# Two mixers with dense steps moved ahead of four products, and the first split block of a feed-forward half in another PSUM bank

## The chip, the cores and the metric

One core of one Trainium2 chip runs the whole program in one launch. The metric is the device time in microseconds, the median of the runs of a kernel. Engines are named as in the profile: PE (TensorE's matmuls), PEld (its weight loads), DVE (VectorE), ACT (ScalarE), POOL (GpSimd), SP (SyncE, which here only issues loads).

## The reference, cut to what matters

Two layers on 256 positions of width 1024, in float32. Each layer is a gated feed-forward half, a token mixer, and a second gated feed-forward half, each after a root-mean-square norm that the conditioning vector scales and shifts.

```python
for l in range(DEPTH):
    h = adaln_pre(x, norm_g[l, 0], shift, scale)
    x = x + 0.5 * gate * swiglu(h, ffn1_w13[l], ffn1_w2[l])
    h = adaln_pre(x, norm_g[l, 1], shift, scale)
    p = dict(zip(names, jnp.split(h @ w_in[l] + b_in[l], splits, axis=-1)))
    y = concat(rms_norm(nsa_mixer(...)), rms_norm(short_conv_mixer(...)), gated_deltanet(...), mlstm_mixer(...))
    x = x + gate * (y @ w_out[l])
    h = adaln_pre(x, norm_g[l, 2], shift, scale)
    x = x + 0.5 * gate * swiglu(h, ffn2_w13[l], ffn2_w2[l])
```

The feed-forward width is 2816, 22 blocks of 128. The mixer has four head groups: sparse attention, a short convolution, a gated delta rule (which needs the inverse of a triangular matrix), and an mLSTM.

## The kernel before, in words

**Feed-forward halves** (class `Half`). Features lie on the partitions and the 256 positions on the free axis. Each block f has three weight tiles of 128x1024: two for the up products (parts 0 and 1) and one for the down product (part 2). A weight tile w is split into a rounded high part `w_..h` (ACT, `high`) and a rest `w_..l` (DVE or POOL, `low`), and a product is three matmuls (`mm3`): high by high, high by low, low by high. The first three blocks of a half (`PRE`) are made unsplit, before the norm's root is known, in the six banks `e0` to `e5`; the root comes through the products `ms` (sum of squares) and `rs` (the roots spread over the partitions), and DVE multiplies it in afterwards (`rooted`: `sl<-e,rsS`). Block 3 (`self.pre`) is the first split block, `ab3`; it is the first pass of the loop in `run`. Each pass there loads and splits the weights of block f+2, runs the 48 matmuls of `ab{f}`, gates it (`gated`: ACT's SiLU `sl<-ab`, then DVE's product `sl<-sl,ab`, then the split into `g`), and adds earlier blocks into the four output banks `y0` to `y3` (`down`: 24 matmuls of a block, six in each bank, in the order y0, y1, y2, y3). The first pass adds block 0. The seam from one half or mixer to the next comes four times: into the first half (`first=True`), and into three others, where `first` is false.

**PSUM banks.** There are eight, in three groups: `c` and `y` with three each, `ab` with two. A tile takes a bank of its group that is free, and its first writer waits until the last readers of the bank's former tile are done. At the three later seams `e0`, `e1`, `e2` are in `c`, `e3` and `e4` in `ab`, `e5`, `ms` and `rs` in `y`. The outputs `y0`, `y1`, `y2` are in `y`, and `y3` is in `ab`.

**What sets the order.** Through the mixers and the seams each engine is held to the order in which the code is written (`InOrder.switch(True)`). The loop in `run` is outside of that: there the framework that builds the program lays the instructions itself, by its own estimate of durations and with the written order as the priority, and each engine then runs its list in that order.

**The mixer** (`mixer`). Its small products depend on chains of small DVE and ACT operations. Between them the code puts pieces of dense work: `step(name, n)` issues the next n products of the input projection (`dq`, `dk`, `c` and so on) or of the output projection (`W3`), 128x128 by 128x256 in float32. The profile counts each such product as two matmul rows. `placed_on_all(name)` reads a finished bank out; for `W3.0` to `W3.3` (four steps each) that is two DVE operations on `xT`. The places that the change touches are lines 1417 (`p_bc`), 1562 (`kq(3)`, `kq(2)`, `scored(0, 0)`), 1654 (`decay_d(0)`), 2043 (`step("W3", 3)`), 2070 (`turned_y(1)`) and 803 (the bank of `ab{f}`). All instructions pass through one recording helper, so every row has line 198.

Of the kernel before, what the change touches and what calls it, by code (L numbers as in the profile page):

```python
# [181 lines left out]
def trunk(ctx: ExitStack, tc: tile.TileContext, a: dict, out: bass.AP, dbg=None):  # L182
# [34 lines left out]
    def mm(o, lhsT, rhs, start=True, stop=True):  # L217
        return pe.matmul(o, lhsT, rhs, start=start, stop=stop, skip_group_check=True)
# [3 lines left out]
    def P(name, tag):  # L222
        return pp.tile([128, 512], F32, tag=tag, bufs=PBUFS[tag], name=name)

    def TT(name, tag, dtype=F32):
        return wk.tile([128, 512], dtype, tag=tag, bufs=BUFS[tag], name=name)
# [67 lines left out]
    def C(n):  # L294
        o, s = CO[n]
        return cst[:, o:o + s]
# [82 lines left out]
    def ada_step(n=1, after=None, q=pool, each=False, tag="ty"):  # L379
        for _ in range(n):  # L380
            ada_load(q, tag)
            ada_use(after, each)
# [182 lines left out]
    def grown(p, l, s, d):  # L565
        c = d % 2
        dve.scalar_tensor_tensor(xT[:, d], p[:, c * T:c * T + T], modG[:, l, s, d:d + 1], xT[:, d],
                                 op0=ALU.mult, op1=ALU.add)
# [27 lines left out]
    class Half:  # L596
# [200 lines left out]
        def run(self, n_ada, first=False):  # L797
            FT = ("c", "ab", "c", "c") if first else ("c", "c", "ab", "c")
            done = 0
            for f in range(self.pre, NF):  # L800
                self.unit(f + AHEAD, range(2))
                self.unit(f + AHEAD, range(2, 3), pool)
                p = P(f"ab{f}", FT[f % 4])
                for half in range(2):
                    for k in range(KD):
                        self.up(f, p, half, k, start=(k == 0))
                g = self.gated(f, p)
                i, m = f - self.pre - 1, NF - 5 - self.pre
                ada_step(n_ada * (i + 1) // m - n_ada * i // m if 0 <= i < m else 0, g, sync if first else pool)
                if first and f in LATE:  # L810
                    LATE[f](g)
                if f == self.pre:
                    self.y = [P(f"y{i}", "y" if i < 3 else "ab") for i in range(4)]
                while done < max(f - 1 - (f == self.pre), 0) and done < NF - TAIL:
                    for d in range(8):
                        self.down(done, d)
                    done += 1
            while done < NF - TAIL:
                for d in range(8):
                    self.down(done, d)  # L820
                done += 1
# [3 lines left out]
    def mixer(l, a1, a2):  # L825
# [40 lines left out]
        def hf(t, u):  # L866
            return t[:, u * T:u * T + T]

        def v2(t):
            return t.rearrange("p (j t) -> p j t", j=2)  # L870
# [4 lines left out]
        def hr(u):  # L875
            return slice(64 * u, 64 * u + 64)
# [27 lines left out]
        def placed_on(n, u, o):  # L904
            nonlocal tok, kr, qr, DQ, DK, og, zb, zS, cs, bs
            m = n + str(u)
            if n == "k":
                kr = TT("kr", "tp") if u == 0 else kr
                biased(hf(kr, u), o, ("ksw", "kvc")[u])
            elif n == "aq":  # L910
                qr = TT("qr", "tp") if u == 0 else qr
                biased(hf(qr, u), o, m)
            elif n == "dq":
                DQ = TT("DQ", "tp") if u == 0 else DQ
                biased(hf(DQ, u), o, m)
            elif n == "dk":
                DK = TT("DK", "tp") if u == 0 else DK
                dve.tensor_scalar(hf(DK, u), o, bcol(m), 0.125, op0=ALU.add, op1=ALU.mult)
            elif n == "o":
                og = TT("og", "tp") if u == 0 else og  # L920
                tanh_half(hf(og, u), o, m)
            elif n == "z":
                zb, zS = (TT("zb", "td"), TT("zS", "tp")) if u == 0 else (zb, zS)
                biased(hf(zb, u), o, m)
                tanh_half(hf(zS, u), o, m)
            elif n == "c":
                cs = TT("cs", "tp") if u == 0 else cs
                biased(hf(cs, u), o, m)
            elif n == "x":
                dve.scalar_tensor_tensor(upad[:, u, 2:], o, bcol(m), hf(cs, u), op0=ALU.add, op1=ALU.mult)  # L930
            elif n == "b":
                bs = TT("bs", "tp") if u == 0 else bs
                biased(hf(bs, u), o, m)
# [54 lines left out]
        def step(name, n=1):  # L988
            if name not in going:
                going[name] = dense(name)  # L990
            for _ in range(n):
                next(going[name], None)
# [11 lines left out]
        def placed_on_all(n):  # L1004
            p = held["banks"].pop(n)
            if n[0] == "W":
                i = int(n[-1])
                grown(p, l, 1, 2 * i)
                grown(p, l, 1, 2 * i + 1)
            elif n == "h":  # L1010
                held["hidS"] = wk.tile([128, 512], F32, tag="hid", bufs=1, name="hidS")
                act.copy(held["hidS"], p)
            else:
                for u in range(2):
                    placed_on(n, u, hf(p, u))
# [30 lines left out]
        def taps(n, u):  # L1046
            j = 2 * "kqv".index(n) + u
            gp, o = held["gp" + n], hf(cvs[n], u)
            w = PA(l, "gconv")[:, 4 * j:4 * j + 4]
            dve.tensor_scalar(o, gp[:, u, 0:T], w[:, 0:1], None, op0=ALU.mult)  # L1050
            for i in range(1, 4):
                dve.scalar_tensor_tensor(o, gp[:, u, i:i + T], w[:, i:i + 1], o, op0=ALU.mult, op1=ALU.add)
# [10 lines left out]
        def kq(h):  # L1063
            r = hr(h % 2)
            p = held["kq", h] = P(f"kq{h}", "c")
            mm(p, KQ[r, h // 2, 0, 0:128], KQ[r, h // 2, :, :])
# [12 lines left out]
        def kr_scaled(u):  # L1079
            for q in range(2):  # L1080
                h = 2 * q + u
                dve.scalar_tensor_tensor(AP1[:, h], held["kr", u][:, q], Dk[:, 1, h:h + 1],
                                         seg1[:, h, None, :].to_broadcast([128, 2, 128]), op0=ALU.mult, op1=ALU.mult)
# [110 lines left out]
        def scored(b, t):  # L1194
            K, n = KB[:, b], 128 * (t + 1)
            for u in range(2):
                held["s", b, t, u] = P(f"s{b}{t}{u}", "y")[:, :2 * n].rearrange("p (q s) -> p q s", q=2)
            for q in range(2):
                for u in range(2):
                    mm(held["s", b, t, u][:, q], qT[hr(u), q, t * 128:t * 128 + 128], K[hr(u), :n])  # L1200
# [213 lines left out]
        placed_on_all("k")  # L1414
        act.copy(glh, gl)

        p_bc = P("bc", "y")
        mm(p_bc[:, 0:8], C("ut"), lf.rearrange("p t h -> p (t h)"), stop=False)
        mm(p_bc[:, 4:8], ones, lf[:, 0], start=False)
        step("dq0")  # L1420
        step("dq1", 4)
        step("dq1")
        taps("k", 1)
        step("dq1")
# [136 lines left out]
        for b in range(2):  # L1561
            act.copy(KB[hr(1 - b), b], KB[hr(b), b])
        kr_scaled(0)
        kq(3)
        kq(2)
        scored(0, 0)
        step("c1", 2)
        taps("v", 1)
        kr_scaled(1)
        placed_on_all("b")  # L1570
# [69 lines left out]
        def decay_d(q):  # L1640
            p = P(f"mw{q}", "y")
            for u in range(2):
                h = 2 * q + u
                for i in range(2):
                    mm(p[:, u * T:u * T + T], identR[:4, h:h + 1].to_broadcast([4, 128]), nMs[i], start=(u == 0 and i == 0), stop=False)
            mm(v2(p)[:, :, 0:128], identR, negR[:, None, :].to_broadcast([128, 2, 128]), start=False)
            held["mw", q] = p

        def decayed(q):
            for u in range(2):  # L1650
                h = 2 * q + u
                act.activation(W0[:, h], held["mw", q][:, u * T:u * T + T], AF.Exp, bias=aa[:, 0, h:h + 1])

        decay_d(0)
        inv_r(1)
        turned(0, 1, 1)
        step("dk0")
        inv_u(0)
        inv_n(1)
        step("dk0")  # L1660
# [379 lines left out]
        for t in range(2):  # L2040
            act.activation(F(f"tmpn{t}", "ta"), acc[:, t * T:t * T + T], AF.Square, accum_out=ss[:, t:t + 1])
        step("W3")
        step("W3", 3)
        p_u2 = P("u2", "c")
        for h in range(4):
            mm(p_u2[:, 64 * h:64 * h + 64], Tt[1][:, h * 128:h * 128 + 128], vp[:, 1, h])
# [8 lines left out]
        def turned_y(t):  # L2055
            p = held["yAT", t] = P(f"yAT{t}", "y")
            for u in range(2):
                tr(p[:, u * 128:u * 128 + 128], acc[:, t * T + u * 128:t * T + u * 128 + 128], ident)
# [7 lines left out]
        for h in range(4):  # L2066
            mm(oC[:, 64 * h:64 * h + 64], AP0[h // 2][:, h % 2, 1, 0:128], U[:, 0, h])
            mm(oC[:, T + 64 * h:T + 64 * h + 64], AP0[h // 2][:, h % 2, 1, 128:], U[:, 0, h], stop=False)
            mm(oC[:, T + 64 * h:T + 64 * h + 64], AP1[:, h, 1, :], U[:, 1, h], start=False)
        turned_y(1)  # L2070
        placed_on_all("W3.1")
        step("W3", 4)
        sqo = TT("sqo", "tc")
        act.activation(sqo, oC, AF.Square)
        xo = SM([128, 2, 4], "xo", "smc")
# [4 lines left out]
        dve.tensor_tensor(v8(no), v8(oC), ro[:, :, :, None].to_broadcast([128, 2, 4, 64]), op=ALU.mult)  # L2080
        placed(1)
        dump("yA", yA)
        step("W3", 4)
        turned_y(0)
        p_oc = turn_back(no, "oCt", "c")
        placed(0)
# [116 lines left out]
```

## Time and profile before

| | |
|---|---|
| median of 3 runs | 1202.23 us |
| the runs | 1198.28, 1202.23, 1204.82 us |
| the profiled execution's own time | 1201.21 us |
| its span | 1199.4 us |
| mean granted TensorE clock | 0.997 |
| PE busy | 1169.1 us (97% of the span) |
| DVE, ACT, POOL busy | 68%, 39%, 23% |

The span runs from the first instruction to the last; the 1.8 us around it are part of the time. PE is busy in nearly all of the span, so the table is read by what PE waits for. A time in the trace is microseconds from the span's start. In a row of the timeline the first two numbers are start and duration, and what stands in brackets is the idle time of that engine just before and what ended it. The mixers lie at about 222 to 418 us and 804 to 1001 us, the three later seams at 418 to 446, 612 to 639 and 1001 to 1029 us.

### The profile page before, as it was taken

The page shows a single profiled execution, that of the slowest core. Times are in us where ns is not written, and L with a number is a line of the kernel's source. Part 1 is how long each engine was busy: PE and PEld are TensorE (multiplying, and loading weights), DVE is VectorE, ACT ScalarE, POOL GpSimd, SP SyncE. Part 2 cuts the span into 40 slices and gives each one's busy share as a digit, 9 for nine tenths or more (in the row PEclk, how much of TensorE's full clock was granted, in tenths as well). Part 3 has the DMA queues.
Part 4 walks back from the last instruction along what each step waited for, and adds up shares of the span by engine and source line. Part 5 has one row for each costly group of instructions (what it writes and reads, how often), then busy time and mean ns, then how long its engine had stood idle before and what let it go on. Part 6 is the DMA issues. An engine that isn't in the chain of part 4 may idle for free.

```text
span 1199.4 us, 21138 instructions
## 1 busy us (share of the span) xinstructions
PE 1169.1 (97%) x8374; PEld 1081.3 (90%) x8374; DVE 815.9 (68%) x1543; ACT 472.7 (39%) x829; POOL 276.9 (23%) x233
## 2 busy tenths in 40 slices
PE   4899999999999999999999999999999999999998
PEld 4799999977779889999999999998866998999998
DVE  6678976358877568888647777734796774765653
ACT  4444454222322354444445444432122334544441
POOL 0023323102100133343321334230201002332321
PEclk9999999999999999999999999999999999999999
DMA  9899985566564338988646787655656532666551
GB/s 327 315 318 329 365 306 190 178 223 195 195 244 140 121 123 288 311 313 291 224 173 229 248 280 265 211 212 176 211 176 248 173 123 71 224 236 228 179 192 50
DMA packets 75444, 266.96 MB, mean 223 GB/s; under 512 B 8559, under 2 KB 9839, under 8 KB 75201
## 3 DMA queue, kind: packets, MB, share of 16 engines
q1 hardware_dynamic: 66096, 232.52, 56.0%
q0 software_dynamic: 8960, 32.88, 8.4%
q8 instruction: 66, 1.08, 0.3%
q14 instruction: 34, 0.28, 0.1%
q10 hardware_dynamic: 288, 0.19, 0.1%
HBM read 264.50 MB, written 2.24 MB: 222 GB/s over the span
## 4 chain that ended last, share of the span: by engine, by line
PE 87%; DVE 7%; DMA 3%; ACT 1%; issue 1%; SPq 0%; DVEq 0%; ACTq 0%
PE ab L198 34%; PE y L198 20%; PE e L198 8%; PE po L198 2%; PE p_td L198 2%; PE pw L198 2%; DVE aw L198 2%; PE hid L198 1%; PE p_o L198 1%; PE p_dk L198 1%; DMA we<-in_ffn_dram 1%; PE p_z L198 1%; PE p_aq L198 1%; DMA aw<-in_adaw_dram 1%; PE p_x L198 1%; PE pv L198 1%
## 5 line engine op out<-in xcount | busy, mean ns | idle before, releaser
L198 DVE SCALAR_TENSOR_TENSOR aw<-aw,cond 128x1024 f32<-128x1024 f32 x144 | 252.0, 1750 | 8.8 <-DMA aw<-in_adaw_dram 8.7
L198 POOL TENSOR_TENSOR w_2l<-w,w_2h 128x1024 fp32r<-128x1024 f32 x71 | 175.0, 2464 | 355.6 <-ACT w_2h L198 349.1
L198 PE MATMUL y<-g,w_2h 128*128 128x256 f32 x1408 | 256.5, 283 | 0.0
L198 PEld LDWEIGHTS y<-g,w_2h 128*128 128x128 f32 x1408 | 218.9, 191 | 0.9 <-issue 0.9
L198 PE MATMUL y<-g,w_2l 128*128 128x256 f32 x704 | 199.2, 283 | 0.0
L198 PE MATMUL ab<-hH,w_0h 128*128 128x256 f32 x600 | 168.8, 281 | 1.3 <-DVE sl L198 1.3
L198 PE MATMUL ab<-hH,w_0l 128*128 128x256 f32 x600 | 168.7, 281 | 0.1
L198 PE MATMUL ab<-hH,w_1l 128*128 128x256 f32 x600 | 168.5, 281 | 0.0
L198 PE MATMUL ab<-hH,w_1h 128*128 128x256 f32 x600 | 168.0, 280 | 0.0
L198 PE MATMUL ab<-hL,w_0h 128*128 128x256 f32 x600 | 167.0, 278 | 0.0
L198 PE MATMUL ab<-hL,w_1h 128*128 128x256 f32 x600 | 166.8, 278 | 0.0
L198 PEld LDWEIGHTS y<-g,w_2l 128*128 128x128 f32 x704 | 134.9, 192 | 0.1
L198 DVE TENSOR_TENSOR w_1l<-w,w_1h 128x1024 fp32r<-128x1024 f32 x75 | 98.5, 1313 | 53.2 <-ACT w_1h L198 52.4
L198 ACT CAST w_2h<-w 128x1024 fp32r<-128x1024 f32 x88 | 91.7, 1047 | 109.1 <-PE ab L198 103.8
L198 ACT CAST w_1h<-w 128x1024 fp32r<-128x1024 f32 x75 | 79.0, 1053 | 119.0 <-PE ab L198 96.5
L198 PEld LDWEIGHTS ab<-hH,w_0h 128*128 128x128 f32 x600 | 113.1, 188 | 2.1 <-issue 2.1
L198 PEld LDWEIGHTS ab<-hL,w_0h 128*128 128x128 f32 x600 | 113.1, 188 | 0.0
L198 PEld LDWEIGHTS ab<-hH,w_0l 128*128 128x128 f32 x600 | 112.6, 188 | 0.3 <-DVE w_0l L198 0.3
L198 PEld LDWEIGHTS ab<-hH,w_1h 128*128 128x128 f32 x600 | 112.8, 188 | 0.0
L198 PEld LDWEIGHTS ab<-hL,w_1h 128*128 128x128 f32 x600 | 112.8, 188 | 0.0
L198 PEld LDWEIGHTS ab<-hH,w_1l 128*128 128x128 f32 x600 | 112.6, 188 | 0.0
L198 DVE TENSOR_TENSOR sl<-sl,ab 128x256 f32<-128x256 f32 x75 | 31.5, 420 | 107.6 <-ACT sl L198 107.6
(444 smaller groups left out, 1887.6 us busy)
## 6 DMA issues: line engine op xcount, KB each, us to landing
w<-in_ffn_dram SPq DMA_DIRECT2D x238, 512.0 KB, 4.4
aw<-in_adaw_dram SPq DMA_DIRECT2D x88, 512.0 KB, 5.0
aw<-in_adaw_dram POOLq DMA_DIRECT2D x56, 512.0 KB, 5.0
we<-in_ffn_dram SPq DMA_DIRECT2D x18, 512.0 KB, 4.4
wh<-in_cw_dram SPq DMA_DIRECT2D x16, 512.0 KB, 3.6
wwo<-in_wout_dram SPq DMA_DIRECT2D x16, 512.0 KB, 3.6
we<-in_ffn_dram SPq DMA_DIRECT2D x16, 256.0 KB, 7.0
wtd<-in_wtd_dram SPq DMA_DIRECT2D x8, 412.0 KB, 5.0
```

Source lines behind the costliest of these rows:

```text
L198: r = f(*args, **kw)
```

## The change

In the first pass of `run`, in the three halves with `first` false, `ab3` takes a bank of the group `y` in place of one of `c`. In both mixers: one step of `dq0` and one of `dq1` go ahead of the products `bc`; the products `s` of `scored(0, 0)` and two steps of `c1` go ahead of `kq(3)` and `kq(2)`; one step of `dk0` goes ahead of `decay_d(0)`; one step of `W3` goes from ahead of the product `u2` to the group ahead of `turned_y(0)` and the product `oCt`, and four steps of `W3` are written ahead of the read-out of `W3.1` rather than behind it. The number of steps stays the same.

```diff
@@ class Half, run
-                p = P(f"ab{f}", FT[f % 4])
+                p = P(f"ab{f}", "y" if f == self.pre and not first else FT[f % 4])
@@ mixer
+        step("dq0")
+        step("dq1")
         p_bc = P("bc", "y")
         mm(p_bc[:, 0:8], C("ut"), lf.rearrange("p t h -> p (t h)"), stop=False)
         mm(p_bc[:, 4:8], ones, lf[:, 0], start=False)
-        step("dq0")
-        step("dq1", 4)
+        step("dq1", 3)
         step("dq1")
@@
         kr_scaled(0)
+        scored(0, 0)
+        step("c1", 2)
         kq(3)
         kq(2)
-        scored(0, 0)
-        step("c1", 2)
         taps("v", 1)
@@
+        step("dk0")
         decay_d(0)
         inv_r(1)
         turned(0, 1, 1)
-        step("dk0")
         inv_u(0)
@@
         step("W3")
-        step("W3", 3)
+        step("W3", 2)
         p_u2 = P("u2", "c")
@@
         turned_y(1)
+        step("W3", 4)
         placed_on_all("W3.1")
-        step("W3", 4)
         sqo = TT("sqo", "tc")
@@
         placed(1)
-        step("W3", 4)
+        step("W3", 5)
         turned_y(0)
         p_oc = turn_back(no, "oCt", "c")
```

## Rows read from the trace of the kernel before

**Rows 1.** The page: span, and busy time of the engines.
```profile
span 1199.4 us, 21138 instructions
PE 1169.1 (97%) x8374; PEld 1081.3 (90%) x8374; DVE 815.9 (68%) x1543; ACT 472.7 (39%) x829; POOL 276.9 (23%) x233
```

**Rows 2.** The waits of PE: waiter, releaser, us in total, times, longest.
```profile
PE kq L198 <- DVE AP L198: 1.3, 2, 0.7
PE ab L198 <- DVE sl L198: 1.3, 2, 0.7
PE oCt L198 <- DVE no L198: 1.1, 2, 0.5
PE bc L198 <- DVE lf L198: 0.8, 2, 0.5
PE mw L198 <- DVE nMl L198: 0.8, 2, 0.4
```

**Rows 3.** Timeline of PE at the seam after the first mixer.
```profile
440.66 0.35 PE L198 MATMUL ab<-hH,w_0h 128*128 128x256 f32 x1 [0.66 <-DVE sl L198]
...
446.35 0.40 PE L198 MATMUL y<-g,w_2h 128*128 128x256 f32 x2
```

**Rows 4.** Timeline of DVE behind that seam.
```profile
449.69 3.82 DVE L198 TENSOR_TENSOR w_2l<-w,w_2h 128x1024 fp32r<-128x1024 f32 x2 [0.67 <-ACT w_2h L198]
453.43 0.41 DVE L198 TENSOR_TENSOR sl<-sl,ab 128x256 f32<-128x256 f32 x1
453.76 1.22 DVE L198 TENSOR_TENSOR w_2l<-w,w_2h 128x1024 fp32r<-128x1024 f32 x1
```

**Rows 5.** The tile sl from 440 to 456 us: duration ns min/median/max.
```profile
L198 DVE SCALAR_TENSOR_TENSOR sl<-sl,sh x3: 470/470/2325, 441.6 to 444.0; 128x256 f32<-128x256 f32 x3
```

**Rows 6.** Timeline of DVE behind the other two seams: the product that ends ab3.
```profile
642.07 0.41 DVE L198 TENSOR_TENSOR sl<-sl,ab 128x256 f32<-128x256 f32 x1
...
1035.88 0.41 DVE L198 TENSOR_TENSOR sl<-sl,ab 128x256 f32<-128x256 f32 x1
```

**Rows 7.** The chain that ended last: start us, us, what.
```profile
642.11 5.66 PE ab L198 x48
...
1028.96 2.87 PE y L198 x24
1031.84 5.66 PE ab L198 x48
```

**Rows 8.** Timeline of PE in the first half's start.
```profile
41.42 5.84 PE L198 MATMUL e<-hF,we 128*128 128x256 f32 x18 [4.31 <-ACT hF L198]
```

**Rows 9.** Busy time by stretch: PE, PEld, DVE, ACT, POOL, granted clock, DMA share, GB/s.
```profile
41.40:47.00 5.60, 5.58 (x18) 4.63 (x19) 5.11 (x11) 2.57 (x7) 0.00 (x0) 0.70 0.90 302
```

**Rows 10.** Timeline of DVE and PE around the products bc, first mixer.
```profile
271.66 0.16 DVE L198 TENSOR_SCALAR lf<-sp 128x8 f32<-128x8 f32 x1
...
271.88 0.39 PE L198 MATMUL bc<-lf,cst 128*128 128x8 f32 x2 [0.51 <-DVE lf L198]
```

**Rows 11.** Timeline of PE and DVE around the products kq, first mixer.
```profile
288.66 1.13 PE L198 MATMUL kq<-KQ 64*128 64x512 f32 x4
...
297.34 0.69 PE L198 MATMUL kq<-KQ 64*128 64x512 f32 x1 [0.67 <-DVE AP L198]
...
308.42 0.88 DVE L198 SCALAR_TENSOR_TENSOR E<-s,ra_y,BT 128x256 f32<-128x256 f32 x2 [0.64 <-PE s L198]
```

**Rows 12.** Timeline of PE at decay_d(0), first mixer.
```profile
320.58 0.38 PE L198 MATMUL mw<-nMh,cstR 4*128 4x256 f32 x1
```

**Rows 13.** Timeline of DVE and PE around the product oCt, first mixer.
```profile
397.69 0.87 DVE L198 SCALAR_TENSOR_TENSOR xT<-pw,modG,xT 128x256 f32<-128x256 f32 x2
...
399.46 3.62 PE L198 MATMUL pw<-yD,wwo 128*128 128x256 f32 x16
...
400.07 0.69 DVE L198 TENSOR_REDUCE xo<-sqo 128x8 f32<-128x512 f32 x1 [1.50 <-ACT sqo L198]
...
403.83 0.66 PE L198 MATMUL oCt<-cst,no 128*128 128x128 f32 x4 [0.53 <-DVE no L198]
```

## The prediction

> **What bounds the kernel now.** I read the page first: PE is busy in 1169.1 of 1199.4 us [rows 1], so nearly all of the time is PE's own work, and a change that only reorders work can win no more than PE waits. The second view is the list of PE's waits [rows 2]. Five of them are on DVE inside the stretches that the change touches: kq 1.3, ab 1.3, oCt 1.1, bc 0.8 and mw 0.8 us, each over two places. Together that is 5.3 us, and it is the most that the change can win: 0.44% of the time. What can be told from no change here is about 0.5%, 6.0 us of the median of 1202.23. The third view is the timeline at each place, to see what is late next.
>
> The sum is made against the profiled execution, 1201.2 us (span 1199.4 and 1.8 around it). It lies 1.0 below the median of the three runs, well inside their scatter.
>
> **The bank of ab3: what it removes.** At the seams after the two mixers the first matmul of ab3 waits 0.66 us for DVE to read e0, whose bank it takes [rows 2, 3]. In the group y the banks of ms and rs have long been read, so the wait goes: 1.3 us together. At the seam between the layers there is no such wait, and nothing to win.
>
> **The bank of ab3: what it adds.** The group y has three banks, and y0, y1 and y2 are to take all three in the same pass. One of them now belongs to ab3 until DVE's product `sl<-sl,ab` has read it. So the third output bank, y2 (matmuls 13 to 18 of block 0's 24), has a new wait: on the gating of ab3. Before the change nothing waited for that product.
>
> How late is it? At the first seam y0 starts at 446.35 [rows 3] and would start 0.66 earlier. A down matmul takes 2.87 us / 24 = 0.12 [rows 7]. y0 and y1 are done 1.4 us after the start, at 447.1. The product on ab3 runs at 453.43 for 0.41 us [rows 4] and ends at 453.84; with the 0.14 us between DVE's end and PE's start y2 can begin at 453.98. Nothing in that product's delay depends on PE: it stands on DVE behind a pair of w_2l splits of 3.82 us [rows 4], and before them a gate of 2.33 us [rows 5].
>
> What does PE do meanwhile? PE runs its list in order, and here the list is the scheduler's, not the written one: on DVE `sl<-sl,ab` runs ahead of the third w_2l [rows 4], which is written before the loop. So I expect y3, whose bank is in another group, and matmuls of ab4 ahead of y2, as many as the scheduler thinks fit before the product ends. If it plans with durations of operations that run alone, it is too early by what the shared work costs on the chip: the gate takes 2.33 in place of 0.47 [rows 5], 1.86 too much, and the pair 3.82 in place of 2 x 1.22 [rows 4], 1.4 too much. It would then plan the product's end for about 453.84 - 3.3 = 450.5, and PE would stand from 450.5 on the clock of before (449.9 on its own, being 0.66 ahead) until 453.98. Against before that is a loss of 453.98 - 450.5 = 3.5 us, the 0.66 already used up.
>
> The bounds: if all 48 matmuls of ab4 (5.66 us [rows 7]) go ahead of y2, the wait is hidden and 0.66 is won; if y2 keeps its place behind y1, PE stands from 447.1 on, or 447.8 on the clock of before, and loses 6.2. I take 3.5, since the planned place rests on rows of the same stretch. At the second mixer's seam the product starts at 1035.88 and the down matmuls at 1028.96 [rows 6, 7], the same distance within 0.2 us: 3.4. Between the layers the product ends at 642.48 and ab4 starts at 642.11 [rows 6, 7], with no such contention: 0.2. Sum 7.1 us (bounds -1.3 and +13). Nothing absorbs it: behind the seam PE runs without waits to the half's end, so a late PE stays late.
>
> **The clock.** In the first half PE waited 4.3 us, up to 41.42 [rows 8], and in the 5.6 us after it the granted clock was 0.70 in the mean [rows 9]: between full (2.4 GHz) and half (1.2 GHz) that is 3.4 us at half, 1.7 us of work lost. The two new waits would be about 4.1 us each, just below that. Ends 0 and 3.4; I take one loss in the two, 1.7, because the nearest row is a little longer than they are.
>
> The Trainium skill, TensorE: Matmul & The Clock Gate, Part 1, goes further: half rate is the array's default, and an idle stretch brings it back. The trace agrees after the wait of rows 8. By that rule both waits would pay, 3.4 in place of 1.7.
>
> **bc.** PE waits 0.51 us for lf in the first mixer [rows 10], 0.3 in the second by the total [rows 2]. Two steps now go ahead; eight cost 3.62 [rows 13], so two take 0.9 and cover the wait: 0.8 won. dq1 was next in any case and its weights are there. DVE reads bc only after other work, so nothing becomes late.
>
> **kq.** kq(2) waits 0.67 for its bank, which DVE still reads [rows 11]; with s and two steps of c1 ahead (over 1.3 us) that wait is covered. kq(3) and kq(2) also come next to each other, as the pair kq(1), kq(0) does, whose four rows take 1.13 us together [rows 11], against 0.69 for a single row: so PE may gain up to 1.3 there. But it runs into the next wait: mw waits 0.4 for nMl already [rows 2], an operation that stands on DVE behind one long run of work. PE can gain past that point only what DVE gains, and DVE's one idle spot between is the 0.64 us in which it waits for s of scored(0, 1) [rows 11]. So 0.6 for each mixer, 1.2 together; bounds 0 and 2.6.
>
> **dk0.** The products mw of decay_d(0) start with no wait marked [rows 12]; the wait mw of rows 2 is at another place, so a step ahead of them covers nothing. 0. If the cover were missing behind it, inv_u(0) would wait at most the one step, 0.45: bounds -0.9 and 0.
>
> **oCt.** One step (0.45) goes from ahead of u2 to ahead of oCt, which waits 0.53 for no [rows 13]. That alone would win 0.4. But u2 and all behind it come 0.45 earlier with only seven steps done, so the eighth, the last that W3.1 needs, now falls behind turned_y(1): it runs in the first 0.45 us of the row of sixteen, 399.01 to 399.46 (that row starts 0.45 earlier than 399.46). On DVE the read-out of W3.1 is still ahead of the reduction xo, so it moves from 397.69, where it filled idle time, to about 399.6, and takes 0.87 [rows 13]. The reduction starts at about 400.45 in place of 400.07, and the chain of small operations to no, and oCt, follow 0.4 later. PE has the same number of steps ahead of oCt and gets there at the same time. The wait grows from 0.53 to 0.9: 0.4 lost in each mixer, 0.8 together; bounds 0.8 lost and 0.9 won.
>
> **Sum.** 1201.2 + 7.1 (banks) + 1.7 (clock) - 0.8 (bc) - 1.2 (kq) + 0 (dk0) + 0.8 (oCt) = 1208.8 us. Without loss of clock 1207.1, with both 1210.5.
>
> **Rivals.** *ab4 hides the wait* (chance 0.16), the one on the other side: not slower. Its place is the list of PE behind y1. y2's first matmul would come at or after 453.9 if nearly the whole of ab4 goes ahead; the deciding point is how late the scheduler believes the product on ab3 to be, and it is from about 45 of the 48 matmuls on that the loss is under 0.4 us. For it: the product's true end, 453.84, is 6.1 us behind PE's arrival at y2, and a scheduler that knew it would fill all of that. Against: the excess of rows 4 and 5 comes from work on other engines at the same time. Time: 1201.2 - 1.3 - 0.8 - 1.2 + 0.8 = 1198.7, and 1196 if oCt also wins what its step covers and the mw wait goes.
>
> *y2 keeps its written place* (chance 0.08): the matmuls of y3 and ab4 stay behind it, and each of the two waits costs 6.2, the third about 2; both clocks fall. 1201.2 + 14.4 + 3.4 - 1.2 = 1218. Against it is the order on DVE in rows 4.
>
> *Both clocks fall* (chance 0.15): the forecast with 1210.5; for it the one row of its length [rows 8, 9].
>
> *The change does not do what it says* (chance 0.06): ab3 gets the bank of e5, which DVE reads last, or the mixers' waits only move. The two effects then cancel, near 1201.
>
> **How the numbers follow.** The forecast has what is left, 0.55, and its own range is 1206 to 1211. The range to 1213 holds it, the fallen clocks and the last rival; left out are the hidden wait (0.16) and the kept place (0.08), less what run-to-run scatter brings in: 1201 to 1213. Slower by over 0.5% (above 1208.2): about 0.6 of the forecast, nearly all of the fallen clocks and of the kept place, 0.56. Within 0.5%: 0.41. Faster by more needs more than all of the 5.3 us: 0.03.
>
> **What would show it.** Right: PE rows of y with a new wait "DVE sl" of 3 to 5 us at two places, after y3 and some of ab4; no wait of ab3 on DVE sl; bc and kq without waits; mw's wait on nMl longer than 0.4; oCt's wait about 0.9, with the reduction directly behind xT on DVE; a granted clock below 1 behind the seams. Wrong: y2 without a wait, or all of ab4 ahead of it.

## The result, and the profile after

The changed kernel takes 1211.05 us (median of five runs, 1209.27 to 1214.56) against 1202.23 before: ratio 1.0088, 95% interval 1.0073 to 1.0103 (the ratio goes by the means, 1211.51 and 1201.20; the two medians alone would give 1.0073). One execution of 3721 us (the bank alone, below) and one of 1295 us (before, below) lie far outside all others and are left out of the medians and ratios here. The forecast was 1208.8 in a range of 1201 to 1213, slower by more than 0.5% with a chance of 0.56. The profiled execution is the one of 1211.05, with a span of 1209.3.

First the list of PE's waits of the changed kernel (waiting engine and tile, releaser, total us, times, longest), which answers to [rows 2]:

```profile
PE ms L198 <- DVE sq L198: 11.4, 1, 11.4
PE y L198 <- DVE sl L198: 8.8, 2, 4.4
PE e L198 <- ACT hF L198: 5.4, 2, 3.8
PE rs L198 <- DVE msr_y L198: 2.2, 1, 2.2
PE mw L198 <- DVE nMl L198: 2.0, 2, 1.0
PE oCt L198 <- DVE no L198: 1.9, 2, 0.9
PE ab L198 <- DVE w_1l L198: 0.4, 1, 0.4
```

bc, kq and the wait of ab for DVE's sl have left the list. In their place stands a new line, y waiting for sl, 8.8 us over two places; and mw and oCt wait longer than before.

The timeline of the changed kernel at those places (start, us, engine, line, operation, out<-in, shape, count, wait ahead of it and its releaser):

```profile
309.91 0.32 PE L198 MATMUL mw<-nMl,cstR 4*128 4x128 f32 x1 [1.00 <-DVE nMl L198]
...
399.38 0.88 DVE L198 SCALAR_TENSOR_TENSOR xT<-pw,modG,xT 128x256 f32<-128x256 f32 x2 [1.89 <-PE pw L198]
400.18 0.68 DVE L198 TENSOR_REDUCE xo<-sqo 128x8 f32<-128x512 f32 x1
...
403.95 0.63 PE L198 MATMUL oCt<-cst,no 128*128 128x128 f32 x4 [0.93 <-DVE no L198]
...
448.88 2.45 POOL L198 TENSOR_TENSOR w_2l<-w,w_2h 128x1024 fp32r<-128x1024 f32 x1 [2.75 <-ACT w_2h L198]
449.79 3.77 DVE L198 TENSOR_TENSOR w_2l<-w,w_2h 128x1024 fp32r<-128x1024 f32 x2 [0.67 <-ACT w_2h L198]
453.47 0.41 DVE L198 TENSOR_TENSOR sl<-sl,ab 128x256 f32<-128x256 f32 x1
453.93 0.54 PE L198 MATMUL y<-g,w_2h 128*128 128x256 f32 x2 [4.37 <-DVE sl L198]
...
647.15 0.41 DVE L198 TENSOR_TENSOR sl<-sl,ab 128x256 f32<-128x256 f32 x1
647.62 0.51 PE L198 MATMUL y<-g,w_2h 128*128 128x256 f32 x2
...
1040.81 0.50 PE L198 MATMUL y<-g,w_2h 128*128 128x256 f32 x2 [4.41 <-DVE sl L198]
```

Read 449.79 to 453.93 together: DVE's pair of splits, the product on ab3 right behind it, and y2 0.05 us after that product's end. (The rows print y without its number; that these are y2's follows from the order in the code and from the wait for sl.) It is the same at 1040.81, where the product ends at 1040.76. Between the layers (647.15, 647.62) y2 also starts right behind the product, but PE had work until then. The chain of waits at that middle seam shows the order (start, us, engine and tile, count):

```profile
644.31 2.29 PE y L198 x18
646.61 1.06 PE ab L198 x9
647.67 0.93 PE y L198 x6
648.60 4.60 PE ab L198 x39
```

Eighteen matmuls of y (y0, y1, y3), nine of ab4, then y2's six and the other 39 of ab4. At the first and the last seam 14 of ab4 stand ahead of y2, and 34 behind it.

The windows of the changed kernel at the seams and in the first mixer (stretch, length, busy time of PE, its weight loads, DVE, ACT and POOL with counts, the granted clock, DMA share, GB/s):

```profile
309.00:310.00 1.00, 0.09 (x1) 0.09 (x1) 1.00 (x4) 0.00 (x0) 0.00 (x0) 1.00 0.93 381
...
311.00:314.00 3.00, 3.00 (x13) 2.81 (x14) 2.35 (x6) 2.12 (x7) 0.00 (x0) 0.50 0.84 315
...
449.50:453.90 4.40, 0.06 (x1) 0.00 (x0) 4.09 (x3) 1.48 (x3) 1.83 (x1) 1.00 0.66 230
453.90:455.00 1.10, 1.07 (x6) 1.07 (x7) 0.42 (x1) 0.41 (x1) 0.00 (x0) 0.67 0.91 209
455.00:457.00 2.00, 2.00 (x11) 2.00 (x11) 0.73 (x1) 1.04 (x1) 0.00 (x0) 0.50 0.88 317
...
462.00:464.00 2.00, 2.00 (x19) 2.00 (x18) 2.00 (x3) 0.94 (x2) 0.00 (x0) 1.00 0.35 96
...
1040.81:1047.20 6.39, 6.39 (x40) 6.39 (x41) 2.88 (x3) 2.50 (x3) 0.00 (x0) 0.73 0.78 253
```

While PE waits at the seam, the granted clock is still 1.00 (2.4 GHz); with its first matmuls after the wait it falls to 0.50 (1.2 GHz), and PE, 100% busy, issues 11 matmuls in 2 us, against 19 in the 2 us from 462 on. It falls behind both long waits, and in the first mixer behind the wait of only 1.00 for nMl; behind the same wait in the second mixer, 1.01, it doesn't. Added up over windows of 1 us, one less the granted clock makes 1.71 us for each fall. PE's time lost is a little less. In the row from 1040.81, y2's six matmuls and 34 of ab4 take 6.39 us; at the middle seam, with no fall, 45 such matmuls take 5.53, so 40 about 4.9. The fall costs PE about 1.5 us there. The second mixers of the runs below that have the same steps show the same: with a fall they last 197.02 (the mixers' edits alone) and 196.98 (the pair on POOL), without one 195.50 (the changed kernel) and 195.48 (block 0 after ab4).

Where the 9.9 us of span went, by marks of the chain of waits in both kernels (each mark is the start of the same group of matmuls):

| stretch | before | after | difference | of that, clock (estimate) |
|---|---|---|---|---|
| to the first mixer (e x40) | 221.71 | 221.32 | -0.39 | 0 |
| first mixer (to e x24) | 196.59 | 197.07 | +0.48 | 1.5 |
| second half of layer 0 | 193.62 | 198.60 | +4.98 | 1.5 |
| first half of layer 1 | 192.43 | 192.79 | +0.36 | 0 |
| second mixer | 196.40 | 195.50 | -0.90 | 0 |
| second half of layer 1 | 198.65 | 204.02 | +5.37 | 1.5 |

Without the clock the three seams cost 3.5 + 0.4 + 3.9, about 7.7 us, and the mixers win 1.0 + 0.9 = 1.9; the clock costs about 4.5.

### The profile page after: what moved, and what is told of

Same layout as the page of the kernel before. It is cut to its first block, busy times and chain, and to the rows that moved or that the text cites. A ratio compares the mean times of both kernels' runs of the same rounds, so it can differ in the third digit from the quotient of the medians.

```text
span 1209.3 us, 21143 instructions
## 1 busy us (share of the span) xinstructions
PE 1171.9 (97%) x8374; PEld 1085.5 (90%) x8374; DVE 810.3 (67%) x1543; ACT 473.3 (39%) x829; POOL 276.6 (23%) x233
## 4 chain that ended last, share of the span: by engine, by line
PE 84%; DVE 8%; DMA 4%; ACT 2%; issue 2%; SPq 0%; DVEq 0%; ACTq 0%
PE ab L198 31%; PE y L198 19%; PE e L198 8%; PE po L198 2%; DMA w<-in_ffn_dram 2%; PE p_td L198 2%; DVE aw L198 2%; PE pw L198 2%; DMA aw<-in_adaw_dram 2%; PE hid L198 1%; PE p_o L198 1%; PE p_dk L198 1%; DVE w_1l L198 1%; PE p_dq L198 1%; PE p_z L198 1%
## 5 line engine op out<-in xcount | busy, mean ns | idle before, releaser
L198 DVE SCALAR_TENSOR_TENSOR aw<-aw,cond 128x1024 f32<-128x1024 f32 x144 | 246.7, 1714 | 7.3 <-DMA aw<-in_adaw_dram 7.2
L198 DVE TENSOR_TENSOR w_1l<-w,w_1h 128x1024 fp32r<-128x1024 f32 x75 | 101.1, 1348 | 53.6 <-ACT w_1h L198 52.7
```

What stands on the lines that cost most here:

```text
L198: r = f(*args, **kw)
```

## The experiments

Nine kernels tell the parts and causes apart; two of them are candidates for a faster version as well. Each was compared with the kernel before on the same chip. A kernel is one of the edits below on before or on the change; "the mixers' edits" are the change without the line of the bank.

**The line of the bank alone.**

```
-                p = P(f"ab{f}", FT[f % 4])
+                p = P(f"ab{f}", "y" if f == self.pre and not first else FT[f % 4])
```

> Only the bank of ab3 is changed; the mixers are those of before. Theory (the slowdown is the third output bank waiting for the gating of ab3): the three seams lose what they lost in the whole change, 5.0, 0.4 and 5.4 us, so +10.7 on before, about 1213 us; y2 waits about 4.4 us for DVE's product at the first and the last of the three seams and under 0.5 at the middle one, and the granted clock falls to 0.50 behind both long waits. Rival (the moved steps shift DVE's work into the seams and lose part of it): under 1207, y2's waits shorter.

Measured: 1212.83 us, ratio 1.0087 (1.0071 to 1.0104), the whole of the slowdown. Of its PE waits, and of its windows those in and behind the last wait:

```profile
PE y L198 <- DVE sl L198: 8.8, 2, 4.4
```

```profile
1041.00:1042.00 1.00, 0.00 (x0) 0.00 (x0) 1.00 (x2) 0.00 (x0) 0.00 (x0) 0.50 0.91 250
...
1042.00:1048.00 6.00, 5.44 (x26) 5.45 (x27) 2.87 (x5) 2.49 (x3) 0.00 (x0) 0.51 0.74 236
```

The same two waits with untouched mixers: the rival falls. At the last of them the clock fell while PE still waited (the window from 1041, without a matmul) and stayed at 0.50 until 1047.6. By granted clock that is 3.41 in place of 1.71; PE took 7.15 us from y2 to the end of ab4 (1042.56 to 1049.71) in place of 6.39, so 0.76 more. In this execution the three halves lose 6.21, 0.59 and 6.13, more than the 5.0, 0.4 and 5.4 expected: this fall is in the last, and the first has a wait of 1.22 at the layer's boundary (617.61), behind a transfer, that the changed kernel's execution doesn't have.

**The mixers' edits alone**, bank of before.

> Only the steps of the mixers are moved; the bank is that of before. Theory (each edit is capped by the next wait, and the W3 steps cost 0.4 a mixer): the second mixer 0.9 us shorter, the first 0.5 longer if the clock falls there again at the wait for nMl and 1.2 shorter if it doesn't, so 1200 to 1202 us. Rival (all five waits of before are won): -2 to -4, 1198 to 1200. Rival (the moved steps also cost at the seams): over 1204. The wait of mw for nMl 1.0, of oCt for no 0.9 in both mixers.

Measured: 1201.53 us, ratio 1.0002 (0.9990 to 1.0015): no change that can be told. mw waits 1.0 and oCt 0.9 in both mixers, as expected. But the second mixer, expected 0.9 shorter, is 0.62 longer (197.02 against 196.40): the clock fell in both mixers this time. The same steps without a fall, the second mixer of the changed kernel, last 195.50, 0.90 shorter than before. So the edits do win about 1 us in a mixer, and a fall takes that back and half a microsecond more. The halves are as before within 0.1 us.

**The whole change, with output block 0 after ab4** in the later halves.

```
-                while done < max(f - 1 - (f == self.pre), 0) and done < NF - TAIL:
+                while done < max(f - 1 - (f == self.pre) * (1 if first else 2), 0) and done < NF - TAIL:
```

> The whole change, and the first pass of the later halves adds no output block, so that all 48 matmuls of ab4 (5.66 us) stand between ab3 and y0. Theory (the loss is the time that PE has nothing to do while ab3 is gated): y2 comes at about 453.0 on the first seam's clock for a product that ends at 453.8, so its wait is 4.4 -> about 1.2 us, too short for the clock to fall; 3.2 us and 1.7 of clock are won back at each of two seams, 1211.05 - 9.8 = about 1201. Rival (the bank costs in another way than by this wait, as by order or sharing further behind): stays above 1207.

Measured: 1202.10 us, ratio 1.0011 (0.9999 to 1.0022). The timeline of PE at the first seam:

```profile
445.40 0.39 PE L198 MATMUL ab<-hH,w_0l 128*128 128x256 f32 x1 [0.24 <-POOL w_0l L198]
...
453.19 0.50 PE L198 MATMUL y<-g,w_2h 128*128 128x256 f32 x2 [0.54 <-DVE sl L198]
```

The bank is the changed one, ab3 doesn't wait, and the wait for the product is 0.54: with ab4 between, 48 matmuls cover the product on ab3, the clock stays at 1.00 at the seams, and all but about 1 us is back. The three halves are 1.15, 0.22 and 0.53 longer than before, where the change had lost 4.98, 0.36 and 5.37; of the 1.15, 0.91 is a wait at the layer's boundary (612.39) behind a transfer. So nearly all of the loss was PE having nothing to do, and nothing further behind. The wait is shorter than the expected 1.2 because PE got there later: ab4, now right behind ab3, waits 0.24 for POOL's split.

**The other way round: ab3 in y, and y2 in c**, with the mixers of before.

```
-            FT = ("c", "ab", "c", "c") if first else ("c", "c", "ab", "c")
+            FT = ("c", "ab", "c", "c") if first else ("c", "c", "ab", "y")
...
-                    self.y = [P(f"y{i}", "y" if i < 3 else "ab") for i in range(4)]
+                    self.y = [P(f"y{i}", ("y" if i < 3 else "ab") if first else ("y", "y", "c", "ab")[i]) for i in range(4)]
```

> The bank of before's mixers, but two groups trade: ab3 (and every fourth block) in y, and the third output bank in c instead of y, in the later halves. So ab3 takes the bank of the spread roots and y2 takes one that was read long ago. Theory: neither ab3's 0.66 nor y2's 4.4 is waited for, the two seams after the mixers win 0.66 each, no clock falls: about -1.3, 1201 us. Rival (the wait returns further behind, where ab7 or ab8 finds its group one bank smaller): 1204 or more. Rival (something else than y2's bank makes ab3 in y slow): 1207 or more.

Measured: 1201.35 us, ratio 1.0003 (0.9994 to 1.0013), not the 1.3 us that two waits of 0.66 would give. Neither ab3 nor y2 waits, at any seam, and no clock falls. But the timeline some 20 us behind the first seam has

```profile
456.95 1.05 ACT L198 CAST w_1h<-w 128x1024 fp32r<-128x1024 f32 x1 [4.12 <-DMA w<-in_ffn_dram]
...
459.00 0.39 PE L198 MATMUL ab<-hH,w_0h 128*128 128x256 f32 x1 [0.51 <-ACT w_0h L198]
...
460.45 0.38 PE L198 MATMUL ab<-hH,w_0l 128*128 128x256 f32 x1 [0.95 <-DVE w_0l L198]
```

ab5 waits 1.46 us for its split weights, and those for a transfer: ACT has been idle 4.12 us for it. In the kernel before, ACT waits for the same transfer too (3.33 us) and PE comes to ab5 hardly before its weights. From the second mixer's end on, where no such wait of over 0.32 follows, the half is 0.38 shorter (198.27 against 198.65). So the 0.66 of ab3 at the first seam was not there to be won in this execution: behind it the transfer of block 5's weights sets the time. The two rivals, 1204 or more and 1207 or more, fall.

**bc, kq and dk0 without W3's steps**, bank of before.

> The moved steps of bc, kq and dk0 without those of W3, bank of before. Theory (the W3 steps cost 0.4 a mixer, since they hold W3.1's read-out ahead of the reduction): the wait of oCt goes back to 0.53, each mixer is 0.4 shorter than in the run with all the mixers' edits, so 196.6 us with a fall of the clock at nMl and 194.9 without; 1199 to 1201 in all. Rival (the step ahead of oCt helps): a mixer 0.4 longer than there.

Measured: 1200.43 us, ratio 0.9995 (0.9984 to 1.0007). In the profiled execution no clock fell in a mixer, and the mixers are 195.09 and 195.10. Second mixers with W3's steps and without a fall are 195.50 (the whole change) and 195.48 (output block 0 after ab4), so leaving W3's steps out wins the 0.4 that was expected. Its timeline and windows at the places of the changed kernel's first fences:

```profile
310.18 0.32 PE L198 MATMUL mw<-nMl,cstR 4*128 4x128 f32 x1 [0.99 <-DVE nMl L198]
...
402.20 0.66 PE L198 MATMUL oCt<-cst,no 128*128 128x128 f32 x4 [0.53 <-DVE no L198]
```

```profile
311.00:314.00 3.00, 3.00 (x23) 2.29 (x23) 2.65 (x7) 1.84 (x5) 0.00 (x0) 1.00 0.85 320
```

The same wait as in the changed kernel, 0.99, and behind it the clock holds: 23 matmuls in 3 us against 13. Its twelve times fit two cases as well, though only one of them has a trace: the two fastest, 1196.50 and 1197.99, ran at mean clocks of 0.999 and 0.998; the other ten are between 1199.71 and 1203.14, at 0.994 to 0.997.

**W3's steps alone**, bank of before.

```
-        step("W3", 3)
+        step("W3", 2)
...
-        placed_on_all("W3.1")
         step("W3", 4)
+        placed_on_all("W3.1")
...
-        step("W3", 4)
+        step("W3", 5)
```

> The W3 steps alone, bank of before. Theory: oCt waits 0.9 in place of 0.53 in both mixers, everything else as before: each mixer 0.4 longer, 197.0 and 196.8 us, +0.8 in all, and no fall of the clock in either mixer. Rival (the step covers the wait, as it reads): oCt waits 0.1, each mixer 0.4 shorter.

Measured: 1202.15 us, ratio 1.0007 (0.9994 to 1.0020), too little to tell by time, but the stretches tell it: 196.95 and 196.76, each 0.36 longer than before, with no fall of the clock in either. Its timeline:

```profile
400.57 0.88 DVE L198 SCALAR_TENSOR_TENSOR xT<-pw,modG,xT 128x256 f32<-128x256 f32 x2 [1.89 <-PE pw L198]
401.36 0.68 DVE L198 TENSOR_REDUCE xo<-sqo 128x8 f32<-128x512 f32 x1
...
405.13 0.63 PE L198 MATMUL oCt<-cst,no 128*128 128x128 f32 x4 [0.93 <-DVE no L198]
```

DVE is idle 1.89 us until PE has finished W3.1, reads it out, and only then reduces: the wait grows from 0.53 to 0.93. PE has as many steps ahead of oCt as before, so the step put there covers nothing of what the same edit made late.

**nMl earlier on DVE**, with bc, kq and dk0, without W3's steps.

```
+        dve.tensor_tensor(nMs[1], negM, nMs[0].bitcast(F32), op=ALU.subtract)
         scored(0, 1)
         biases(0, 1, 0)
...
-        dve.tensor_tensor(nMs[1], negM, nMs[0].bitcast(F32), op=ALU.subtract)
         squares("q")
```

> As the run without the W3 steps, and DVE's subtraction for nMl is written ahead of scored(0, 1), 13 lines earlier. Theory (what the kq edit wins is capped by mw's wait for nMl, and that wait of 1.0 is what the clock falls behind): mw doesn't wait, no clock falls, each mixer gains 0.5 (bc) to 0.3, 0.7 to 1.3 (kq) and 0.4 (mw): 1.4 to 2.2 each, so 194.2 to 195.0 us a mixer and -3 to -4 in all. Rival (PE then waits for the next product of DVE, as W1's or turned's): mixers over 195.5. Rival (the clock falls for another reason, the run of matmuls with 4 partitions): 0.50 still stands behind mw.

Measured: 1195.55 us (1194.77 to 1196.95), ratio 0.9954 (0.9940 to 0.9969): 0.46% faster than before, an interval that doesn't reach 1, and so faster than both kernels. Its PE waits and the window at mw:

```profile
PE ms L198 <- DVE sq L198: 11.4, 1, 11.4
PE e L198 <- ACT hF L198: 3.6, 2, 2.0
PE rs L198 <- DVE msr_y L198: 2.2, 1, 2.2
PE ab L198 <- DVE sl L198: 1.3, 2, 0.7
PE oCt L198 <- DVE no L198: 1.0, 2, 0.5
PE ab L198 <- DVE w_1l L198: 0.5, 1, 0.5
```

```profile
308.00:312.00 4.00, 4.00 (x36) 3.06 (x28) 3.96 (x10) 0.45 (x2) 0.00 (x0) 1.00 0.87 279
```

The mixers are 193.88 and 193.93, 2.71 and 2.47 shorter than before and over 2.2, the most that was expected. Against the kernel without this line they win 1.2 each beside the clock, which is the wait of 1.0 and 0.2 more. No other product of DVE takes its place: both rivals fall. How much moving nMl would win without the other edits was not run.

The first mixer as one window, in the kernel before and in this one:

```profile
221.71:418.30 196.59, 194.47 (x1102) 158.57 (x1102) 131.48 (x396) 56.69 (x148) 22.67 (x34) 1.00 0.53 178
...
220.98:414.86 193.88, 193.36 (x1102) 158.29 (x1102) 131.34 (x396) 56.49 (x148) 22.82 (x34) 1.00 0.54 180
```

Of the 2.71 us, 1.60 was idle time of PE (2.12 to 0.52), the waits of bc, kq and mw. The other 1.11 was counted as busy (194.47 to 193.36): the same 1102 matmul rows, in another order, are busy for less.

**That, with the two groups traded.**

> The one before, and the two groups traded for ab3 and y2. Theory (behind the first seam the weights of ab5 set the time, so that the 0.66 won there is waited for at 458 to 461): as the run without the trade, within 1 us, with a wait of 0.5 to 1.5 of ab5 on its split weights; the last seam wins about 0.4. Rival (the wait for ab5's weights in the run of the trade alone was a late transfer of that execution): 1.3 faster than without the trade.

Measured: 1196.68 us, ratio 0.9960 (0.9945 to 0.9974), not to be told from the one before. ab5 waits 0.44 at 458.38, less than the 0.5 expected; the first seam is 0.45 shorter (47.92 us from e x24 to the y that before has at 466.75, against 48.37 without the trade). The last seam doesn't win its 0.4: ab3 no longer waits there, but ab5 does, and the half is 0.18 longer than without the trade (198.81 against 198.63).

```profile
1039.04 0.39 PE L198 MATMUL ab<-hH,w_0l 128*128 128x256 f32 x1 [0.70 <-DVE w_0l L198]
```

At the layer's boundary y waits 0.73 for DVE (637.95), behind a transfer that ACT was idle for. The trade wins at most half a microsecond at the first seam, and in the total nothing that shows.

**The whole change, with the pair of splits on POOL** at the two seams after the mixers.

```
-            a2.unit(f, range(2, 3))
+            a2.unit(f, range(2, 3), pool if f < 4 else dve)
```

> The whole change, and at the two seams after the mixers the two splits w_2l that stand on DVE ahead of the product on ab3 go to POOL. The order on PE changes with it: 5 matmuls of ab4 stand ahead of y2 in place of 14, so PE comes to y2 about 1.1 us earlier. Theory (what sets y2's start is that product, and it stands behind the pair on DVE): DVE is free when ACT's silu of ab3 ends at 450.97 on the clock of the whole change, y2 starts at about 451.5 in place of 453.9, its wait is 4.4 -> about 3; less the 1.1 that is left of ab4 each seam wins 1.4, and 1.7 more if the clock doesn't fall behind 3 us: 1205 to 1208 us. Rival (the product is late for another reason, ACT or the gate before): y2 starts at 453.9 as before, and the time is 1211 or more.

Measured: 1211.82 us, ratio 1.0089 (1.0066 to 1.0112). Its timeline at the first seam and its window behind it:

```profile
448.90 7.30 POOL L198 TENSOR_TENSOR w_2l<-w,w_2h 128x1024 fp32r<-128x1024 f32 x3 [2.75 <-ACT w_2h L198]
...
451.02 0.42 DVE L198 TENSOR_TENSOR sl<-sl,ab 128x256 f32<-128x256 f32 x1 [1.89 <-ACT sl L198]
...
451.50 0.79 PE L198 MATMUL y<-g,w_2h 128*128 128x256 f32 x2 [3.02 <-DVE sl L198]
...
451.97 1.98 DVE L198 TENSOR_TENSOR g<-sl,g 128x256 fp32r<-128x256 f32 x1 [0.53 <-ACT g L198]
```

```profile
451.00:455.50 4.50, 4.00 (x21) 4.00 (x22) 3.81 (x3) 1.45 (x2) 4.50 (x3) 0.62 0.67 229
```

The mechanism came out as written: DVE waits for ACT alone, the product runs at 451.02, y2 starts at 451.50 after a wait of 3.02, and the seam is 1.48 us shorter than in the whole change (51.96 against 53.44), the last half 1.40 (202.62 against 204.02). The time missed, for other reasons: the clock fell behind both waits of 3.0 as behind 4.4, it fell in both mixers where the profiled execution of the change has one fall, and PE waited 1.73 and 0.61 at the boundary of the layers (up to 617.26 and 646.17), where this execution has transfers of weights on its chain. What the product stands behind is shown; that the edit makes the kernel faster is not.

## Why the prediction was right, and where a term was off

**The banks**: forecast 7.1 (3.5, 3.4 and 0.2), measured about 7.7 without the clock (3.5, 3.9, 0.4). The step that carried it, y0, y1 and y3 and some of ab4 ahead of y2 and then a stand, is what PE's rows show, with 14 matmuls of ab4 at the two seams. The bank alone gives all of it, and enough work ahead of y2 takes nearly all of it away. Both rivals about the place of y2 are ruled out: ab4 does not hide the wait, and y2 does not keep its written place. (The bound of +13 was less than the 14.4 that the forecast gave to the kept place; neither came into play.) That the number comes from durations of operations that run alone stays an inference; the run with the pair on POOL fits it (9 matmuls less, 1.1 us, where the pair is out of the way), but no trace shows the plan itself.

**Why the product on ab3 is late** was put to rows 4 and 5, an excess of 1.4 and 1.86. The traces now show where it comes from: both stand beside a split on POOL.

```profile
443.73 2.40 POOL L198 TENSOR_TENSOR w_0l<-w,w_0h 128x1024 fp32r<-128x1024 f32 x1 [2.76 <-ACT w_0h L198]
444.08 2.33 DVE L198 SCALAR_TENSOR_TENSOR sl<-sl,sh 128x256 f32<-128x256 f32 x1 [0.36 <-ACT sl L198]
```

The gate of 2.33 in the changed kernel ends at 446.41, 0.28 after POOL's split w_0l; ACT, idle 2.16 us until that gate is done, then has four casts of weights ahead of ab3's SiLU. As for the pair, POOL splits w_2l until 451.33 (448.88 for 2.45 us), DVE's pair begins at 449.79 and ends at 453.56, which is 451.33 and two splits of 1.22, less 0.2 of overlap. With POOL busy from 448.90 to 456.20, DVE's g<-sl,g takes 1.98 in place of 0.42, while the product, which reads one operand from PSUM, takes its 0.42 beside the same POOL work. The Trainium skill, SBUF — State Buffer, section "SBUF: two separate sides", has the rule for this: a DVE instruction with two SBUF inputs and a GpSimd instruction that reads SBUF share a pair of ports under an exclusive lock, and the later one is blocked for the whole of the other's instruction. These rows agree with it, within 0.2 us for the pair.

**Nothing absorbs it** was right for a loss and wrong for a gain. The 0.66 of ab3 that the forecast took as won at the first seam would have been waited for again at ab5, on the transfer of its weights, as the traded groups showed (ab5 waited 1.46 at the first seam in the one run, 0.44 there and 0.70 at the last in the other). Here it hardly matters to the sum, since y2's loss covers both.

**The clock** is the term that was mis-sized: one fall of 1.7 forecast, three measured, of 1.71 each by granted clock and about 1.5 of PE's time. What came true at the seams is the rival *both clocks fall*, which had a chance of 0.15. Two steps failed. At the seams the row of 4.3 us in rows 8 was taken as the edge, and waits of 4.1 us as just below it; both waits brought a fall, and so did both of 3.0 us later. In the mixers no fall was considered at all, since the wait there grows to only 1.0. The Trainium skill, TensorE: Matmul & The Clock Gate, Part 1, by which both seams would pay, was the better guide there: the trace agrees with it at all four waits of 4.4 us. That the forecast's own sum with both falls, 1210.5, lies so near to 1211.05 is in part luck, since the third fall, in the mixer, is made up by other terms.

**The cap of 5.3 us**, that the change can win no more than PE waits, is wrong as a bound. bc, kq and mw waited 1.3 + 0.8 + 0.8 = 2.9 us before; with nMl moved, the mixers won 2.71 + 2.47 = 5.18, since PE's busy time shrank by 1.11 in the first mixer as well. The forecast had seen this for kq, up to 1.3 for a pair of rows that come together, and still set the cap by the waits.

**bc and kq**: forecast -0.8 and -1.2, together -2.0; measured in the run without W3's steps -1.50 and -1.30, together -2.8. The cap by nMl held: mw's wait grew from 0.41 to 1.00, and DVE got to nMl 1.49 earlier than before (309.73 - 221.59 against 311.34 - 221.71). Of this 0.72 is its idle spot at E, forecast as 0.64. The other 0.77 is bc: DVE starts its long run at 285.10 in place of 285.99, 0.77 earlier from the mixer's start, where the forecast counted the marked wait of 0.51. What the cap held back is 1.2 a mixer, shown by moving nMl.

**dk0**: forecast 0; the time has nothing left over for it, but it was not run alone. **oCt**: forecast 0.4 lost in each mixer, with the read-out of W3.1 ahead of the reduction; measured 0.36 in each, and by that route.

**The sum**: 1201.2 + 7.7 + 4.5 - 1.9 and 0.4 less before the first mixer is 1211.1. The forecast was 2.2 us short. The clock is 2.8 more than forecast and the banks 0.6; the mixers' larger gain (0.7) and the 0.4 before them, which no edit accounts for, made up for part of it.

## What to carry to other kernels

A bank, like a queue, has a next owner: when a tile moves into another group, look for who else is to have that bank in the same pass, and for what must read the tile first. Where PE runs an order made ahead of time, the cover for a late product is the work that stands ahead of its consumer there, so putting a whole block of matmuls in between is worth more than making the product earlier by a microsecond or two. And when a wait is taken away, move the next operand on that path too: the edits of the mixers won nothing that could be measured until nMl was moved (and W3's steps left out), and 0.46% with it. A list of waits bounds neither gain nor loss: it misses the busy time that another order saves, and the wait that the change itself makes.

## What was not expected of the hardware

The granted clock falls behind far shorter waits than the 4.3 us of rows 8. In the profiled executions every wait of 3.0 us or more of y2 went with a fall (six of six), in the run of the bank alone once already while PE still waited. Of the mixers' waits of 1.0 for nMl six of ten were followed by one (changed kernel one of two, mixers' edits two of two, block 0 after ab4 one of two, W3's steps left out none of two, pair on POOL two of two); of the waits of 0.4 at the same place none of eight; where mw doesn't wait none of four. Ahead of this wait PE runs narrow matmuls, hid with 32 columns of weights and mw with 4 rows. By granted clock a fall at these places costs 1.70 or 1.71 us each time, once twice that; PE loses about 1.5 by it. The same mixer with the same wait thus has two lengths, 195.5 and 197.0. What decides between them in an execution stays open.
